# A decoder block whose MLP is computed with seven-product block products: the forms of h2 and z made in the order of the products that read them, the casts of summed weights held back, and the buffers dealt out anew

## The chip, the cores and the metric

The kernel runs on one core of one Trainium2 chip. The metric is the device time of one execution in microseconds (us). Three runs of the kernel before gave 702.37, 704.03 and 705.65 us; their median is 704.03 us. The profile shown here belongs to one further execution, which took 705.45 us by itself.

## The reference, cut to what matters

The input is x with 512 tokens of width 1024, in float32. The first half of the block is a gated merge of differential attention and causal pooling; the change does not touch it. What matters is the end of the layer:

```
x  = x + merged @ w_out                  # 512x1024 @ 1024x1024
h2 = rmsnorm(x, norm_mlp_g)
z  = square(relu(h2 @ w_up))             # 512x1024 @ 1024x4096
x  = x + z @ w_down                      # 512x4096 @ 4096x1024
out = rmsnorm(x, final_norm_g)
```

## The kernel before, in words

**Precision.** Every matrix product is made of three matmuls in the rounded format float32r: each operand is parted into a high part (a cast, made by ScalarE) and a low part (the operand minus its high part, made by VectorE), and hi*hi, hi*lo and lo*hi are added up in PSUM.

**Seven products instead of eight.** The width 4096 of the MLP is taken in four quarters q. For each, `up(q)` multiplies h2 (512 x 1024) by a 1024 x 1024 block of w_up, and `down(q)` multiplies z (512 x 1024) by a 1024 x 1024 block of w_down. Both use a block scheme with seven products of 2x2 blocks in place of eight (Strassen's, in the form with fewer additions). So each operand appears in seven **forms**: for h2 and z these are A11, A12, A22, S1, S2, S3, S4 (S1 to S4 are sums and differences of blocks), for the weights b11, b21, b22 (blocks as they lie in memory) and t1, t2, t3, t4 (sums). The order in which TensorE runs the seven is written out by hand in `up` (lines 702 to 731) and `down` (lines 766 to 778): A11 (m1), then A12 (m2) and S1 (m5) in one order or the other, S2 (m6), S3 (m7), A22 (m4), S4 (m3). Several of them add onto the same two PSUM banks `ma`, with a copy of the banks taken between (`keep`, line 687, on ScalarE in `up`; `to_x1`, line 756, on VectorE in `down`). One product in `up` is 48 matmuls of 256 columns (lines 672, 673, 676), one in `down` is 24 of 512 columns (lines 744 to 746).

**The forms of h2.** Line 580 on: for each of the four token tiles t, w_out's last product is added to x1 (line 560), the row's norm is worked out, h2 is written (line 587), transposed by TensorE (line 593), and its forms are made. Tiles 0 and 1 give A11 and A12; tiles 2 and 3 give, each, A22, S1, S2, S3 and S4 in one go (lines 602 to 611): raw form (`hx`) by ScalarE or VectorE, then `split` (lines 566 and 567) into the high and the low part in `gf`.

**The forms of z.** In `up`, the results of the products are combined into R[0] to R[4] (lines 691 to 730), and `zsplit` (lines 699 and 700) parts each form into `zfh` and `zfl`, two buffers of 28 KB per partition that hold all seven forms. They lie where `hx` and `hbuf` (h2 and its gain) lay before.

**The weights.** `weights` (line 617) is a generator; each product takes its next pair of tiles from it. Raw blocks come by DMA on SyncE's queue into the tiles `wr` (two) and `wal` (two); the sums are built in `wga` (two) and `wal` by VectorE once (line 642) and after that by DMAs that add onto a tile (line 629, issued by GpSimd). `parts` casts a pair to `wh` (ScalarE, line 113) and subtracts for `wl` (VectorE, line 114). `wh` and `wl` have four buffers each, which is two products' worth: a cast for product n has to wait until product n-2 has read its half. For t1, t2 and t4 the same tile `wga` is cast, added to, and cast again.

**Order of the work.** A scheduler places all instructions in each engine's queue at build time, by readiness in a simulated timeline and otherwise by the order of the program; on the chip every engine runs its own queue in that fixed order. `after(a, b)` adds an edge that only places a behind b in that timeline; it is no wait on the chip.

The gain of the last norm is loaded and scaled in `gain` (lines 528 and 529), into the slot that the forms S1 and S2 of h2 leave (line 796).

Of the kernel before, what the change touches and what calls it, by code (L numbers as in the profile page):

```python
# [11 lines left out]
F32 = mybir.dt.float32  # L12
F32R = mybir.dt.float32r
# [39 lines left out]
def block_kernel(ctx, tc, xT, x_tok, gains, pos, consts, w_in, w_v, w_pool, w_out, w_up, w_dn, out):  # L53
# [37 lines left out]
    def f(ap):  # L91
        return ap.bitcast(F32)
# [19 lines left out]
    def split_w(raw, hi, lo, sl=slice(0, 1024), eng=None):  # L112
        ins = A.copy(out=hi[:, sl], in_=raw[:, sl])  # L113
        (eng or G).tensor_tensor(out=lo[:, sl], in0=raw[:, sl], in1=f(hi)[:, sl], op=ALU.subtract)  # L114
        return ins
# [393 lines left out]
    A11, A12, A22, S1, S2, S3, S4 = range(7)  # L509

    x1 = big.tile([P, NT, D], F32, tag="s0", name="x1")
    hbuf = bk.tile([P, 7, 4, HS], F32, tag="zfl", name="hbuf", bufs=1)
    hflat = hbuf.rearrange("p a b c -> p (a b c)")
    h2 = hflat[:, 0 : NT * D].rearrange("p (t d) -> p t d", t=NT)
    hx = bk.tile([P, 7, 4, HS], F32, tag="zfh", name="hx", bufs=1)
    gfs = [big.tile([P, 2, 2, 4, HS], F32R, tag=f"s{i}", name=f"gf{i}") for i in (1, 4, 3)]
    gf7 = bk.tile([P, 1, 2, 4, HS], F32R, name="gf7")
    gf = {}
# [8 lines left out]
    def gain(g, i):  # L527
        nc.sync.dma_start(out=g, in_=gains[i])
        A.mul(out=g, in_=g, mul=-0.5)
        return g  # L530

    def square(t, n, junk):

        A.activation(out=junk, in_=x1[:, t, n * 512 : n * 512 + 512], func=AF.Square, accum_out=st[:, t, n : n + 1])
# [23 lines left out]
    def x1_add(t, n, a_):  # L558
        xs = x1[:, t, n * 512 : n * 512 + 512]
        V.tensor_tensor(out=xs, in0=a_, in1=xs, op=ALU.add)  # L560
        square(t, n, h2[:, t, :512])

    def split(form, sl, src):

        hi, lo = gf[form]
        A.copy(out=hi[:, :, sl], in_=src)  # L566
        V.tensor_tensor(out=lo[:, :, sl], in0=src, in1=f(hi)[:, :, sl], op=ALU.subtract)
# [9 lines left out]
    for t in range(NT):  # L577
        x1_add(t, 0, po[t])
        row_early(t, 0)
    g2b = gain(hflat[:, NT * D : NT * D + D], 0)  # L580
    ws = [get_w(w_out[1, kk], f"o1_{kk}", V if kk % 2 else None) for kk in range(4)]
    for t in range(NT):
        a_ = acc(f"po1_{t}")
        for k in range(NK):
            mm_rows(a_, t, k, ws[k // 2], k == 0, k == NK - 1)
        x1_add(t, 1, a_)
        V.scalar_tensor_tensor(out=h2[:, t], in0=x1[:, t, :], scalar=row_scale(t, 1), in1=g2b, op0=ALU.mult, op1=ALU.mult)
        pv = []
        for b in range(2):
            pt = acc(f"h2T{t}_{b}")  # L590
            for j in range(4):
                k = 4 * b + j
                T.transpose(out=pt[:, j * P : j * P + P], in_=h2[:, t, k * P : k * P + P], identity=ident)
            pv.append(pt.rearrange("p (j q) -> p j q", q=P))
        sl = slice((t % 2) * P, (t % 2) * P + P)
        raw = [hx[:, i, :, sl] for i in range(7)]
        if t < 2:
            for form in (A11, A12):
                A.copy(out=raw[form], in_=pv[form])
                split(form, sl, pv[form])  # L600
        else:
            A.copy(out=raw[A22], in_=pv[1])  # L602
            V.tensor_tensor(out=raw[S1], in0=raw[A22], in1=pv[0], op=ALU.subtract)
            split(S1, sl, raw[S1])
            V.scalar_tensor_tensor(out=raw[S2], in0=raw[S1], scalar=-1.0, in1=raw[A11], op0=ALU.mult, op1=ALU.subtract)
            split(S2, sl, raw[S2])
            V.tensor_tensor(out=raw[S3], in0=raw[A11], in1=pv[0], op=ALU.subtract)  # L607
            split(S3, sl, raw[S3])
            split(A22, sl, raw[A22])
            V.scalar_tensor_tensor(out=raw[S4], in0=raw[S2], scalar=-1.0, in1=raw[A12], op0=ALU.mult, op1=ALU.subtract)  # L610
            split(S4, sl, raw[S4])


    zfh = bk.tile([P, 7, 4, HS], F32R, tag="zfh", name="zfh", bufs=1)
    zfl = bk.tile([P, 7, 4, HS], F32R, tag="zfl", name="zfl", bufs=1)

    def weights(src, q, nm, swap=False):

        def raw(b, tag="wr", pool=wp):
            tiles = [pool.tile([P, 1024], F32, tag=tag, name=f"{tag}_{nm}{b}_{q}_{c}", bufs=2) for c in range(2)]  # L620
            if b is not None:
                for c in range(2):
                    nc.sync.dma_start(out=tiles[c], in_=src[q, b, c])
            return tiles

        def plus(tiles, b):

            for c in range(2):
                G.dma_start(out=tiles[c], in_=src[q, b, c], accum_op=ALU.add)

        def parts(rs, b):
            out_ = []
            for c in range(2):
                hi = wp.tile([P, 1024], F32R, tag="wh", name=f"wh_{nm}{b}_{q}_{c}", bufs=4)
                lo = wp.tile([P, 1024], F32R, tag="wl", name=f"wl_{nm}{b}_{q}_{c}", bufs=4)
                split_w(rs[c], hi, lo, eng=V)
                out_.append((hi, lo))
            return out_

        r11, al, ga = raw(0), raw(1, "wal", bk), raw(None, "wga", bk)  # L640
        for c in range(2):
            V.tensor_tensor(out=ga[c], in0=r11[c], in1=al[c], op=ALU.add)
        yield parts(r11, "b11")
        if swap:
            yield parts(raw(2), "b21")
        plus(al, 3)
        w = parts(ga, "t1")
        plus(ga, 3)
        yield w
        if not swap:  # L650
            yield parts(raw(2), "b21")
        w = parts(ga, "t2")
        plus(ga, 2)
        yield w
        yield parts(al, "t3")
        yield parts(ga, "t4")
        yield parts(raw(3), "b22")

    def up(q):

        W = weights(w_up, q, "u", q == 0)

        def product(form, name, onto=None):
            w, pa = next(W), onto or [acc(f"u{name}{q}_{i}") for i in range(2)]
            rh, rl = gf[form]
            for i in range(2):
                hi, lo = w[i]
                for p in range(2):
                    a_ = pa[i][:, p * HS : p * HS + HS]
                    for k in range(4):  # L670
                        c = slice((p * 4 + k) * P, (p * 4 + k) * P + P)
                        T.matmul(a_, lhsT=hi[:, c], rhs=rh[:, k, :], start=p + k == 0 and onto is None, stop=False, skip_group_check=True)  # L672
                        T.matmul(a_, lhsT=hi[:, c], rhs=rl[:, k, :], start=False, stop=False, skip_group_check=True)  # L673
                    for k in range(4):
                        c = slice((p * 4 + k) * P, (p * 4 + k) * P + P)
                        T.matmul(a_, lhsT=lo[:, c], rhs=rh[:, k, :], start=False, stop=k == 3, skip_group_check=True)  # L676
            return pa
# [18 lines left out]
                A.activation(out=r_, in_=r_, func=AF.Square)  # L696

        def zsplit(form, r):
            A.copy(out=zfh[:, form], in_=r)  # L699
            V.tensor_tensor(out=zfl[:, form], in0=r, in1=f(zfh)[:, form], op=ALU.subtract)  # L700

        ma = product(A11, "m1")
        keep(ma, R[0])
# [12 lines left out]
        z_of(R[1], -1.0)  # L716
        product(A22, "m4", onto=ma)
        z_of(R[3], 1.0, ma)
        V.tensor_tensor(out=R[4], in0=R[0], in1=R[3], op=ALU.subtract)
        V.tensor_tensor(out=R[3], in0=R[1], in1=R[3], op=ALU.subtract)  # L720
        zsplit(S1, R[3])
        V.scalar_tensor_tensor(out=R[0], in0=R[3], scalar=-1.0, in1=R[0], op0=ALU.mult, op1=ALU.subtract)
        product(S4, "m3", onto=mc)
        join(mc, R[2])
        z_of(R[2], -1.0)
        zsplit(A12, R[2])
        zsplit(S2, R[0])
        zsplit(S3, R[4])
        zsplit(A22, R[1])
        V.scalar_tensor_tensor(out=R[2], in0=R[0], scalar=-1.0, in1=R[2], op0=ALU.mult, op1=ALU.subtract)  # L730
        zsplit(S4, R[2])

    def down(q):
        W = weights(w_dn, q, "d")

        def product(form, name, onto=None):

            w, pa = next(W), onto or [acc(f"d{name}{q}_{a}") for a in range(2)]
            for a in range(2):
                for p in range(4):  # L740
                    hi, lo = w[p // 2]
                    sl, tsl = slice((p % 2) * 512, (p % 2) * 512 + 512), slice(a * P, a * P + P)
                    zh, zl = zfh[:, form, p, tsl], zfl[:, form, p, tsl]
                    T.matmul(pa[a], lhsT=zh, rhs=hi[:, sl], start=p == 0 and onto is None, stop=False, skip_group_check=True)  # L744
                    T.matmul(pa[a], lhsT=zl, rhs=hi[:, sl], start=False, stop=False, skip_group_check=True)  # L745
                    T.matmul(pa[a], lhsT=zh, rhs=lo[:, sl], start=False, stop=p == 3, skip_group_check=True)  # L746
            return pa
# [102 lines left out]
```

## Time and profile before

| | |
|---|---|
| three runs | 702.37, 704.03, 705.65 us (median 704.03) |
| the profiled execution | 705.45 us, span from first to last instruction 703.6 us |
| TensorE matmul (PE) busy | 672.5 us, 96% of the span |
| weight loads of TensorE (PEld) | 581.1 us, 83% |
| VectorE (DVE) | 531.8 us, 76% |
| ScalarE (ACT) | 455.3 us, 65% |
| GpSimd (POOL) | 174.5 us, 25% |
| mean granted TensorE clock | 0.989 |
| first matmul of the MLP (line 672) | 357.35 us after the start of the span |
| last matmul | 695.49 us |

PE, DVE, ACT and POOL are the engines; SP is the queue that issues plain DMAs. A row of the timeline has start, duration, engine, line, operation, tiles written and read, shape and count; in square brackets stands how long the engine had been idle and who released it. The end of a matmul in the records is modelled and lies beyond the start of the next one, so the pace of TensorE is read from the distance of two starts, not from the durations.

### The profile page before, as it was taken

To read this page: it belongs to the slowest core of one execution; us is meant where nothing else is said; L and a number is where in the kernel's file an instruction comes from. 1 tells how busy PE (TensorE), PEld (TensorE's weight loads), DVE (VectorE), ACT (ScalarE), POOL (GpSimd) and SP (SyncE) were. 2 spreads that over 40 slices of the span, in tenths; PEclk is the share of its full clock that TensorE was granted. 3 is DMA by queue.
4 is the path that set the end of the run, shared out by engine and by line. 5 is a ranking of instruction groups with operands and counts; after the bars stand their busy time and mean duration, and the time that the engine had idled before them with its cause. 6 is when DMAs were issued, how large, how long until landed. Compare 5 with 4: busy or idle time off the path is not lost.

```text
span 703.6 us, 10026 instructions
## 1 busy us (share of the span) xinstructions
PE 672.5 (96%) x3674; PEld 581.1 (83%) x3674; DVE 531.8 (76%) x852; ACT 455.3 (65%) x735; POOL 174.5 (25%) x167
## 2 busy tenths in 40 slices
PE   9999999999999999999996999999999999999995
PEld 7788788888888887777886987899779987898874
DVE  6953977779798866946588698768966699746995
ACT  7554488986976789565375674368634784366754
POOL 6101634174336434521200010101101010110100
PEclk9999999999999999999998999999999999999998
DMA  8434464335626265254546385786759586595733
GB/s 276 156 117 119 124 146 128 91 88 130 160 71 142 91 143 119 61 216 150 120 128 113 127 195 157 198 221 154 170 156 250 143 206 179 142 231 162 188 88 119
DMA packets 31296, 105.14 MB, mean 149 GB/s; under 512 B 3728, under 2 KB 4368, under 8 KB 31248
## 3 DMA queue, kind: packets, MB, share of 16 engines
q0 software_dynamic: 9792, 35.66, 28.3%
q1 hardware_dynamic: 21456, 68.85, 28.0%
q8 instruction: 29, 0.48, 0.3%
q14 instruction: 19, 0.16, 0.1%
HBM read 102.40 MB, written 2.10 MB: 149 GB/s over the span
## 4 chain that ended last, share of the span: by engine, by line
PE 60%; DVE 15%; DMA 9%; ACT 7%; issue 6%; POOL 2%; SPq 0%; DVEq 0%; ACTq 0%; POOLq 0%
PE um L672 6%; PE um L673 6%; PE um L676 5%; PE dm L745 5%; PE dm L746 4%; PE dm L744 4%; DMA wga_dNone<-w_dn 4%; DVE p L381 2%; PE q L132 2%; PE po L554 2%; PE k L133 2%; PE k L132 2%; PE q L133 2%; PE q L136 2%; PE k L136 2%
## 5 line engine op out<-in xcount | busy, mean ns | idle before, releaser
L672 PE MATMUL um<-gf,wh_ut 128*128 128x256 f32 x256 | 66.4, 291 | 8.0 <-ACT gf L566 6.2
L673 PE MATMUL um<-gf,wh_ut 128*128 128x256 f32 x256 | 66.2, 290 | 0.0
L672 PEld LDWEIGHTS um<-gf,wh_ut 128*128 128x128 f32 x256 | 50.7, 199 | 8.6 <-ACT gf L566 6.6
L745 PE MATMUL dm<-wh_dt,zfl 128*128 128x512 f32 x128 | 50.3, 393 | 3.2 <-DVE zfl L700 3.2
L744 PE MATMUL dm<-wh_dt,zfh 128*128 128x512 f32 x128 | 49.5, 392 | 3.7 <-DVE x L756 3.7
L673 PEld LDWEIGHTS um<-gf,wh_ut 128*128 128x128 f32 x256 | 50.8, 198 | 0.0
L113 ACT CAST wh_ub<-wr_u 128x1024 fp32r<-128x1024 f32 x24 | 25.2, 1054 | 38.1 <-PE dm L745 15.4
L746 PE MATMUL dm<-wl_dt,zfh 128*128 128x512 f32 x128 | 49.2, 390 | 0.0
L672 PE MATMUL um<-gf,wh_ub 128*128 128x256 f32 x192 | 48.1, 283 | 1.1 <-DVE hx L607 1.1
L673 PE MATMUL um<-gf,wh_ub 128*128 128x256 f32 x192 | 48.1, 283 | 0.0
L376 ACT ACTIVATE p<-p,st 128x128 f32<-128x128 f32 (+3 forms) x64 | 35.8, 560 | 17.6 <-DVE st L372 17.1
L113 ACT CAST wh_dt<-wga_dNone 128x1024 fp32r<-128x1024 f32 x24 | 25.3, 1053 | 30.1 <-PE dm L745 14.9
L114 DVE TENSOR_TENSOR wl_ub<-wr_u,wh_ub 128x1024 fp32r<-128x1024 f32 x24 | 29.0, 1223 | 19.7 <-ACT wh_ub L113 19.7
L676 PE MATMUL um<-gf,wl_ut 128*128 128x256 f32 x256 | 42.6, 290 | 0.0
L114 DVE TENSOR_TENSOR wl_ut<-wga_uNone,wh_ut 128x1024 fp32r<-128x1024 f32 x24 | 29.2, 1222 | 17.1 <-ACT wh_ut L113 17.1
L756 DVE TENSOR_TENSOR x<-x,dm 128x512 f32<-128x512 f32 x56 | 37.3, 681 | 6.3 <-PE dm L746 6.3
L113 ACT CAST wh_ut<-wga_uNone 128x1024 fp32r<-128x1024 f32 x24 | 25.1, 1048 | 24.4 <-DMA wga_uNone<-w_up 14.4
L672 PEld LDWEIGHTS um<-gf,wh_ub 128*128 128x128 f32 x192 | 36.8, 192 | 1.4 <-ACT hx L602 1.2
L700 DVE TENSOR_TENSOR zfl<-rawz,zfh 128x1024 fp32r<-128x1024 f32 x28 | 34.1, 1220 | 4.2 <-ACT zfh L699 4.1
L673 PEld LDWEIGHTS um<-gf,wh_ub 128*128 128x128 f32 x192 | 36.8, 192 | 0.2
L676 PEld LDWEIGHTS um<-gf,wl_ut 128*128 128x128 f32 x256 | 36.9, 200 | 0.0
L744 PE MATMUL dm<-wh_db,zfh 128*128 128x512 f32 x96 | 36.8, 390 | 0.0
(279 smaller groups left out, 2114.6 us busy)
## 6 DMA issues: line engine op xcount, KB each, us to landing
wr_u<-w_up SPq DMA_DIRECT2D x24, 512.0 KB, 5.3
wr_d<-w_dn SPq DMA_DIRECT2D x24, 512.0 KB, 3.8
wga_uNone<-w_up POOLq DMA_DIRECT2D x16, 512.0 KB, 6.0
wga_dNone<-w_dn POOLq DMA_DIRECT2D x16, 512.0 KB, 6.0
wr_q<-w_in SPq DMA_DIRECT2D x8, 512.0 KB, 3.2
wr_k<-w_in SPq DMA_DIRECT2D x8, 512.0 KB, 3.3
wr_ga<-w_in SPq DMA_DIRECT2D x8, 512.0 KB, 3.2
wr_gp<-w_in SPq DMA_DIRECT2D x8, 512.0 KB, 3.3
```

What stands on the lines that cost most here:

```text
L113: ins = A.copy(out=hi[:, sl], in_=raw[:, sl])
L114: (eng or G).tensor_tensor(out=lo[:, sl], in0=raw[:, sl], in1=f(hi)[:, sl], op=ALU.subtract)
L132: T.matmul(acc, lhsT=hi[:, c], rhs=rh[:, k, :], start=k == 0, stop=False)
L376: A.activation(out=pr[:, c, :N], in_=pr[:, c, :N], func=AF.Exp, scale=-1.0, bias=st[:, c : c + 1], accum_out=st[:, 2 + c : 3 + c])
L672: T.matmul(a_, lhsT=hi[:, c], rhs=rh[:, k, :], start=p + k == 0 and onto is None, stop=False, skip_group_check=True)
L673: T.matmul(a_, lhsT=hi[:, c], rhs=rl[:, k, :], start=False, stop=False, skip_group_check=True)
L676: T.matmul(a_, lhsT=lo[:, c], rhs=rh[:, k, :], start=False, stop=k == 3, skip_group_check=True)
L700: V.tensor_tensor(out=zfl[:, form], in0=r, in1=f(zfh)[:, form], op=ALU.subtract)
L744: T.matmul(pa[a], lhsT=zh, rhs=hi[:, sl], start=p == 0 and onto is None, stop=False, skip_group_check=True)
L745: T.matmul(pa[a], lhsT=zl, rhs=hi[:, sl], start=False, stop=False, skip_group_check=True)
L746: T.matmul(pa[a], lhsT=zh, rhs=lo[:, sl], start=False, stop=p == 3, skip_group_check=True)
L756: V.tensor_tensor(out=xs, in0=xs, in1=pa[a], op=(ALU.add, ALU.subtract)[n])
```

## The change

It does five things.

1. `hx` and h2 become five tiles of one tag `zf` (8 KB each); h2 holds two token tiles at a time, and the gain g2b lies in a free half of the fourth. In the loop over t, tiles 2 and 3 make only A22 (raw), S1 with its split, and S3 (raw). A new function `form_h2` makes the splits of S2, S3 and A22, and the raw form and split of S4 and S2, right ahead of the product that reads the form, in `up(0)` alone.
2. `zfh` and `zfl` are gone. `zsplit` takes a tile from the same ring `zf` of five for each form, and works in two halves of 512 columns.
3. In `up`, the form S1 of z is made first, in halves, straight into R[4]; S3 (R[0]-R[3]), which stood ahead of it, is made after S2.
4. Every third pair of weight parts lies in two further tiles (`whb`, `wlb`), so that parts for three products exist at once.
5. The casts of t2, t3 and t4 get an edge behind the first matmul of the latest product that has begun in the program (`hold`).

```
+    def zf(name, dt=F32R):
+        return bk.tile([P, 2, 4, HS], dt, tag="zf", name=name, bufs=5)
+
+    hxs = [zf(f"hx{i}", F32) for i in range(4)]
+    h2 = zf("h2", F32).rearrange("p a b c -> p a (b c)")
+    hx = {form: hxs[i // 2][:, i % 2] for i, form in enumerate((A11, A12, A22, S1, S2, S4, S3))}
...
             V.tensor_tensor(out=raw[S1], in0=raw[A22], in1=pv[0], op=ALU.subtract)
             split(S1, sl, raw[S1])
-            V.scalar_tensor_tensor(out=raw[S2], in0=raw[S1], scalar=-1.0, in1=raw[A11], op0=ALU.mult, op1=ALU.subtract)
-            split(S2, sl, raw[S2])
             V.tensor_tensor(out=raw[S3], in0=raw[A11], in1=pv[0], op=ALU.subtract)
-            split(S3, sl, raw[S3])
-            split(A22, sl, raw[A22])
-            V.scalar_tensor_tensor(out=raw[S4], in0=raw[S2], scalar=-1.0, in1=raw[A12], op0=ALU.mult, op1=ALU.subtract)
-            split(S4, sl, raw[S4])
+
+    def form_h2(form):
+
+        for t in range(2):
+            sl = slice(t * P, t * P + P)
+            raw = {i: hx[i][:, :, sl] for i in hx}
+            if form == S2:
+                V.scalar_tensor_tensor(out=raw[S2], in0=raw[S1], scalar=-1.0, in1=raw[A11], op0=ALU.mult, op1=ALU.subtract)
+            if form == S4:
+                V.scalar_tensor_tensor(out=raw[S4], in0=raw[S2], scalar=-1.0, in1=raw[A12], op0=ALU.mult, op1=ALU.subtract)
+            if form in (S2, S3, A22, S4):
+                split(form, sl, raw[form])
...
-        def parts(rs, b):
+        def parts(rs, b, hold=None):
+
+            third = nparts[0] % 3 == 2
+            nparts[0] += 1
...
+                cast = split_w(rs[c], hi, lo, eng=V)
+                if hold:
+                    after(cast, hold)
...
-        w = parts(ga, "t2")
+        w = parts(ga, "t2", first[-1])
         plus(ga, 2)
         yield w
-        yield parts(al, "t3")
-        yield parts(ga, "t4")
+        yield parts(al, "t3", first[-1])
+        yield parts(ga, "t4", first[-1])
...
         def zsplit(form, r):
-            A.copy(out=zfh[:, form], in_=r)
-            V.tensor_tensor(out=zfl[:, form], in0=r, in1=f(zfh)[:, form], op=ALU.subtract)
+            z = zform[form] = zf(f"z{form}_{q}")
+            for i, r_ in enumerate(halves(r)):
+                hi, lo = (z[:, j, 2 * i : 2 * i + 2, :] for j in range(2))
+                A.copy(out=hi, in_=r_)
+                V.tensor_tensor(out=lo, in0=r_, in1=f(hi), op=ALU.subtract)
...
-        V.tensor_tensor(out=R[4], in0=R[0], in1=R[3], op=ALU.subtract)
-        V.tensor_tensor(out=R[3], in0=R[1], in1=R[3], op=ALU.subtract)
-        zsplit(S1, R[3])
-        V.scalar_tensor_tensor(out=R[0], in0=R[3], scalar=-1.0, in1=R[0], op0=ALU.mult, op1=ALU.subtract)
+        for a_, b_, c_ in zip(halves(R[4]), halves(R[1]), halves(R[3])):
+            V.tensor_tensor(out=a_, in0=b_, in1=c_, op=ALU.subtract)
+        zsplit(S1, R[4])
         product(S4, "m3", onto=mc)
         join(mc, R[2])
         z_of(R[2], -1.0)
         zsplit(A12, R[2])
-        zsplit(S2, R[0])
-        zsplit(S3, R[4])
+        V.scalar_tensor_tensor(out=R[4], in0=R[4], scalar=-1.0, in1=R[0], op0=ALU.mult, op1=ALU.subtract)
+        zsplit(S2, R[4])
+        V.tensor_tensor(out=R[0], in0=R[0], in1=R[3], op=ALU.subtract)
+        zsplit(S3, R[0])
         zsplit(A22, R[1])
```

## The prediction on record

> **What bounds the kernel now.** I read the page first, then the waits of TensorE, then its timeline at those places, then the queues of ScalarE and VectorE around them.
>
> ```profile
> span 703.6 us, 10026 instructions
> PEclk9999999999999999999998999999999999999998
> ```
>
> ```profile
> PE um L672 <- ACT gf L566: 6.2, 2, 3.9
> PE dm L744 <- DVE x L756: 3.7, 4, 1.1
> PE dm L745 <- DVE zfl L700: 3.2, 4, 0.8
> PE um L672 <- ACT rawz L687: 1.7, 1, 1.7
> PE um L672 <- DVE hx L607: 1.1, 1, 1.1
> ```
>
> The second line is the granted clock in tenths over 40 slices of the span; it drops in one slice behind the middle, and in the last, where TensorE has ended. The waits (total us, times, longest) hold all that TensorE loses in the MLP: five causes, and everything the diff touches is among their releasers. How much each costs is seen from starts:
>
> ```profile
> 357.35 0.28 PE L672 MATMUL um<-gf,wh_ub 128*128 128x256 f32 x1
> 367.51 0.36 PE L676 MATMUL um<-gf,wl_ub 128*128 128x256 f32 x1
> 368.94 0.36 PE L672 MATMUL um<-gf,wh_ub 128*128 128x256 f32 x1 [1.07 <-DVE hx L607]
> 371.41 0.64 PE L676 MATMUL um<-gf,wl_ub 128*128 128x256 f32 x4
> 374.34 0.50 PE L672 MATMUL um<-gf,wh_ut 128*128 128x256 f32 x2 [2.29 <-ACT gf L566]
> 378.77 0.80 PE L672 MATMUL um<-gf,wh_ut 128*128 128x256 f32 x2 [3.93 <-ACT gf L566]
> 415.64 0.62 PE L744 MATMUL dm<-wh_db,zfh 128*128 128x512 f32 x2
> 417.10 0.50 PE L745 MATMUL dm<-wh_dt,zfl 128*128 128x512 f32 x1 [0.84 <-DVE zfl L700]
> 432.19 0.39 PE L745 MATMUL dm<-wh_dt,zfl 128*128 128x512 f32 x1
> 432.42 0.39 PE L746 MATMUL dm<-wl_dt,zfh 128*128 128x512 f32 x1
> 433.77 0.47 PE L744 MATMUL dm<-wh_dt,zfh 128*128 128x512 f32 x1 [0.96 <-DVE x L756]
> 639.97 0.28 PE L673 MATMUL um<-gf,wh_ut 128*128 128x256 f32 x1
> 640.09 0.64 PE L676 MATMUL um<-gf,wl_ut 128*128 128x256 f32 x4
> 642.47 0.39 PE L672 MATMUL um<-gf,wh_ut 128*128 128x256 f32 x1 [1.75 <-ACT rawz L687]
> 695.49 0.39 PE L746 MATMUL dm<-wl_db,zfh 128*128 128x512 f32 x1
> ```
>
> A matmul of 256 columns starts every 0.12 us (639.97 to 640.09), one of 512 every 0.23 us (432.19 to 432.42; 0.227 over a run of them). So the MLP's pure work is 28 products x 48 x 0.12 = 161.3 us in the four `up` and 28 x 24 x 0.227 = 152.5 us in the four `down`, together 313.8 us. It ran from 357.35 to 695.72 us, 338.4 us. Of the rest, 16 transposes of h2, put at the same 0.12 us each, are 1.9 us. About 22.7 us are lost. TensorE is the bound, and nothing that leaves it these 313.8 us can win more than that.
>
> The loss in five parts, as distance of two starts less one pace:
> - Head, first gap: 368.94 - 367.51 - 0.12 = 1.31 us.
> - Head, second gap: the last of the four matmuls at 371.41 starts at 371.77; until 378.77 only two more start: 7.00 - 3 x 0.12 = 6.64 us.
> - From A11 to S1 in `down`: 417.10 - 415.87 - 0.23 = 1.00, which is 0.16 more than the idle time in the row. Four such waits: 3.2 + 4 x 0.16 = 3.8 us.
> - From S2 to S3 in `down`: 433.77 - 432.42 - 0.23 = 1.12, again 0.16 more. Four: 3.7 + 0.6 = 4.3 us.
> - In the last `up`: 642.47 - 640.45 - 0.12 = 1.90 us.
>
> Two of the gaps cost clock as well (columns: stretch, its length, then busy us and instructions of PE, PEld, DVE, ACT, POOL, then granted clock, DMA share, GB/s):
>
> ```profile
> 371.90:378.70 6.80, 0.65 (x4) 0.30 (x2) 6.80 (x10) 5.19 (x9) 0.86 (x1) 0.89 0.54 96
> 378.70:384.10 5.40, 5.33 (x25) 5.33 (x26) 3.19 (x6) 2.54 (x6) 0.86 (x1) 0.51 0.85 152
> 642.40:647.00 4.60, 4.53 (x25) 4.53 (x26) 3.65 (x4) 3.24 (x6) 0.10 (x1) 0.63 0.29 98
> 415.00:435.00 20.00, 18.20 (x80) 14.37 (x78) 19.51 (x21) 9.78 (x10) 1.73 (x2) 1.00 0.74 189
> ```
>
> After the head's gap the clock is 0.51 and 25 matmuls take 5.4 us in place of 25 x 0.12 = 3.0: 2.4 us. After 642.4 a mean of 0.63 over 4.6 us means 3.4 us at half rate, so 1.7 us. Sum: head 1.3 + 6.6 + 2.4 = 10.3; inside `down` 3.8 + 4.3 = 8.1; the last `up` 1.9 + 1.7 = 3.6. Together 22.0, which fits the 22.7.
>
> **The change part by part.** Why the gaps are there:
>
> ```profile
> 365.25 2.35 DVE L114 TENSOR_TENSOR wl_ut<-wga_uNone,wh_ut 128x1024 fp32r<-128x1024 f32 x2
> 369.92 0.68 DVE L603 TENSOR_TENSOR hx<-hx,h2T 128x512 f32<-128x512 f32 x1
> 372.20 1.04 ACT L113 CAST wh_ut<-wga_uNone 128x1024 fp32r<-128x1024 f32 x1 [2.13 <-DMA wga_uNone<-w_up]
> 376.12 1.04 ACT L113 CAST wh_ut<-wga_uNone 128x1024 fp32r<-128x1024 f32 x1 [1.31 <-DMA wga_uNone<-w_up]
> 430.72 1.05 ACT L113 CAST wh_dt<-wga_dNone 128x1024 fp32r<-128x1024 f32 x1 [2.44 <-DMA wga_dNone<-w_dn]
> 431.80 1.23 DVE L114 TENSOR_TENSOR wl_dt<-wga_dNone,wh_dt 128x1024 fp32r<-128x1024 f32 x1 [0.40 <-ACT wh_dt L113]
> 432.94 1.28 DVE L756 TENSOR_TENSOR x<-x,dm 128x512 f32<-128x512 f32 x2
> 408.96 1.22 DVE L719 TENSOR_TENSOR rawz<-rawz 128x1024 f32<-128x1024 f32 x1
> 410.69 1.22 DVE L720 TENSOR_TENSOR rawz<-rawz 128x1024 f32<-128x1024 f32 x1
> 415.83 1.22 DVE L700 TENSOR_TENSOR zfl<-rawz,zfh 128x1024 fp32r<-128x1024 f32 x1
> 640.89 1.06 ACT L529 ACTIVATE gfb<-gfb 128x1024 f32<-128x1024 f32 x1 [2.44 <-DMA gfb<-gains]
> ```
>
> *Held casts, head.* S1 of the fourth token tile exists raw at 369.92 + 0.68 = 370.6. ScalarE could cast it at once, but stands 2.13 us and again 1.31 us on two casts of t2 whose DMA has not landed; the form's casts lie behind them. With the edge, t2's casts come behind S1's first matmul. Cast and subtraction (0.6 and 0.7 us, a little over half of the rows of 1024 columns) then end at about 372, as A12's matmuls run out at 371.9. The second gap goes but for some tenths, and the half rate with it: 6.6 + 2.4 us. What is late next is t2 itself: cast 1.04 and 1.23 of subtraction per half. Its first half landed at 372.2, so is ready by 374.5; the second landed at 376.1, ready at 378.4. S2 would start at 371.9 + 5.8 = 377.7 and needs the second half at 380.5. It fits by 2 us.
>
> *Later splits.* S2's two raw forms and two splits on VectorE, 4 x 0.68, now stand between S1's first matmul and S2 (5.8 us, in which t2 takes 2 x 1.2 more): 5.1 us, covered with 0.7 us to spare, and by 2.9 us more for t2's second half. S3, A22 and S4 each need 1.4 to 2.7 us in 5.8. Cost 0; without cover TensorE stands for whatever is over 5.8 us.
>
> *First gap of the head.* It ends with line 607 of tile 2, which frees a PSUM bank; the order of VectorE had put 2.35 us of t1's subtraction (365.25) before it. t1 is the third pair, gets the new tiles, and need not wait until A11 is read. So its cast and subtraction move ahead, and 1.3 us go. Bounds: 0 to 1.3 of gain; and those 2.35 us must go somewhere among the norm's rows before 357, where they can delay h2 by up to one subtraction, 1.2 us. I take the whole gain and 0.5 of cost.
>
> *S2 to S3 in `down`.* VectorE stands behind t4's subtraction (431.80), this behind its cast, this 2.44 us behind the DMA; `to_x1`, which frees the bank, begins at 432.94. With the edge, t4's cast is placed behind S3's first matmul, and so behind `to_x1`. Four times gone: 4.3 us. Queued behind a late cast are then its own subtraction and A22, one product (24 x 0.227 = 5.4 us) later; two casts and two subtractions in series need 1.05 + 2 x 1.23 = 3.5 us. Covered.
>
> *A11 to S1 in `down`.* VectorE made S3's difference (408.96) before S1's (410.69), and S1's low part at 415.83. Now S1's is first, by halves: 1.22 us less ahead, the first half need not wait for the second square, and the third tile pair moves t1's subtractions of `down` one product forward. TensorE needs it at 415.9, it came at 417.05. 1.2 us are enough; all four gaps go, 3.8 us.
>
> *Halves.* Two ops of 512 columns take 1.28 us on VectorE (432.94) against 1.22 for one of 1024: 0.06 x 8 = 0.5 us per quarter. ScalarE is busy under half of 415 to 435. Hidden; without cover 2 us in all.
>
> *The ring of five.* z's A22 and S4 wait for A11 and S1 of `down` to be read; they are used four to five products later, over 20 us. h2's two halves: tile 2 waits for tile 0's transposes, a product earlier. Cost 0. Raw DMAs on SyncE's queue and the adding DMAs on GpSimd's are as many as before, some up to a product earlier.
>
> *The gain gfb.* Untouched, so I leave its 3.6 us in: a scale that waits 2.44 us for its DMA stands ahead of `keep` on ScalarE.
>
> Sum: -10.3 - 8.1 + 0.5 = -17.9 us. On the profiled execution 705.45 - 17.9 = 687.5; that execution lies 1.4 above the median, so **686.0 us** against 704.0.
>
> **The rivals.**
> - *The gain's stall goes as well.* Between S2 and S3 ScalarE now has t4's and b22's casts ready, so the scale may be placed behind the first `keep`. For: the row at 640.89 is a matter of place alone. Against: nothing orders it. 686.0 - 3.6 = 682.4. Chance 0.18.
> - *The head is only half mended.* VectorE is busy 6.80 of 6.80 us there, so S1 or S2 may still come 3 us late. Then the gap is 3.0 and the half rate of 2.4 us stays: 686.0 + 5.4 = 691.4. For the clock: 642.47 shows that a gap of 1.9 us is followed by half rate. Chance 0.12. The Trainium skill, TensorE: Matmul & The Clock Gate, section on why this matters, allows gaps up to about 3 us without a drop. By that rule such a rest would cost its 3.0 us alone, 689.0; the trace disagrees, with 3.4 us at half rate behind 1.9 us.
> - *VectorE is the bound where `up` meets `down`.* It is busy 19.51 of 20 us in 415 to 435, and the halves add to it. If S1 comes as late as now and the 0.5 us per quarter show, 3.8 + 2.0 come back: 691.8. Against: the reordering takes 1.22 us from ahead of S1, the halves put 0.2 there. Chance 0.07. The Trainium skill, Perfetto Trace Analysis, section on optimizing Scalar/DVE operations, says to group operations where the engine is saturated and to break them up where it only causes bubbles; VectorE is here both.
> - *The edge does little.* It orders a simulated timeline; if DMAs land there as early as before relative to the products, the casts stay in front of the same instructions. Then only the 3.8 us go: 700.2, no change. Against: the edge hangs on the product, not on the DMA. Chance 0.06.
> - *Slower: raw casts block `keep`.* With three pairs of tiles, casts of b21 and b22 are no longer held back by TensorE's reading, but stand in ScalarE's queue as soon as the simulated DMA lands. Where the real one is over 2.3 us late (half a product, 2.9, less the copy, 0.6), `keep` is late and TensorE stops, as at 640.89, for 3.6 us. Twice in each of four `up`: 686.0 + 8 x 3.6 = 714.8; it turns slower than before from six such stops on. For: the row of the gain. Against: raw blocks are asked for a product earlier. Chance 0.07.
>
> **How the numbers follow.** The forecast has 0.50. About 0.5%, 3.5 us, is what a measurement can tell from no change. Faster: 0.50 + 0.18 + 0.12 + 0.07 = 0.87; same 0.06; slower 0.07. The range takes in the first four cases, 682.4 to 691.8. Below, it gets the scatter of the runs shown (1.7 us) and the 0.5 that I charged: 680. Above, 1.7 of scatter, 0.7 more for t1 and 1.3 for the first gap: 696.
>
> **What would show it.** Right: no wait of line 672 on the casts of h2's forms over 1 us, clock 1.00 from 357 to 640; no waits on z's low part or on `to_x1` in `down`; the first matmul of `up` to the last of `down` in about 320 us (338.4 - 10.3 - 8.1); the stop behind the gain still there. Wrong: ScalarE idle on a DMA with a copy or a split behind it in the queue; new rows of TensorE waiting on `wh` or `wl`; the norm's rows before 357 later by more than 1 us.

## The result, and the profile after

The changed kernel took 711.53 us (median of four runs, 709.98 to 712.71) against 703.90 us (702.37 to 705.65) for the kernel before on the same chip: a ratio of 1.0106, 95% interval 1.0073 to 1.0139. It is about 7.6 us slower, where 18 us of gain were forecast. Its profiled execution took 710.68 us with a span of 708.7 us. The profile of the kernel before comes from an execution of 705.45 us, above its median, so the two profiles differ by 5.2 us and not by 7.6. Lines of the changed kernel are numbered anew: matmuls of `up` 692, 694, 697, of `down` 770, 772, 773; `keep` 708, `z_of` 716 and 717, the two halves of `zsplit` 723 and 724, `to_x1` 783, `split` 569 and 570.

The page of the changed kernel, span and granted clock:

```profile
span 708.7 us, 10061 instructions
PEclk9999999999999999999999999999999999999988
```

Its waits of TensorE in the MLP (total us, times, longest):

```profile
PE dm L770 <- DVE st L542: 4.8, 1, 4.8
PE um L692 <- ACT rawz L708: 3.7, 3, 2.2
PE dm L770 <- DVE x L783: 2.9, 1, 2.9
PE um L694 <- DVE gf L570: 2.6, 1, 2.6
PE dm L772 <- DVE z L724: 1.3, 1, 1.3
PE um L697 <- DVE wl_ut L114: 0.9, 1, 0.9
PE um L692 <- ACT gf L569: 0.8, 1, 0.8
PE dm L773 <- DVE wl_dt L114: 0.4, 1, 0.4
```

The eight regular waits in `down` (four on z's low part, four on `to_x1`) are gone from this list, and so is the stop behind the gain. In their place stand single stops, fewer and longer. The rows at which TensorE resumes, and the stretches behind three of them (columns of the second fence as in the prediction):

```profile
371.38 0.50 PE L692 MATMUL um<-gf,wh_ut 128*128 128x256 f32 x2 [0.77 <-ACT gf L569]
374.51 0.58 PE L694 MATMUL um<-gf,wh_ut 128*128 128x256 f32 x1 [2.62 <-DVE gf L570]
508.76 0.50 PE L770 MATMUL dm<-wh_dt,z 128*128 128x512 f32 x1 [2.90 <-DVE x L783]
554.07 0.38 PE L692 MATMUL um<-gf,wh_ut 128*128 128x256 f32 x1 [2.18 <-ACT rawz L708]
663.24 0.50 PE L772 MATMUL dm<-wh_db,z 128*128 128x512 f32 x1 [1.31 <-DVE z L724]
679.75 0.76 PE L770 MATMUL dm<-wh_dt,z 128*128 128x512 f32 x1 [4.79 <-DVE st L542]
```

```profile
374.20:377.70 3.50, 3.19 (x15) 3.19 (x16) 3.50 (x6) 3.47 (x8) 0.01 (x1) 0.51 0.00 0
555.10:558.60 3.50, 3.50 (x19) 3.50 (x18) 2.38 (x4) 2.17 (x3) 0.00 (x0) 0.51 0.79 267
679.50:685.00 5.50, 5.25 (x13) 4.18 (x14) 4.42 (x10) 4.10 (x6) 0.00 (x0) 0.51 0.00 0
```

Each stop again costs some 0.16 us more than the idle time in its row. The head: 0.93 + 2.78, and half of 3.2 us at half rate, 1.6: 5.3 us, where there had been 10.3. In `down`: 3.06 + 1.47 + 0.56 + 4.95, and half of 5.25 us, 2.6: 12.6 us, where there had been 8.1. In `up`: `keep` 3.7 + 3 x 0.16, the low part of t1 0.9 + 0.16, and half of 3.5 us, 1.75: 7.0 us, where there had been 3.6. That is 2.9 us more than before, and the measured stretch from the first matmul (357.22) to the last (698.36) agrees: 341.1 us against 338.1. The other 2.2 us of the span come behind the last matmul (10.3 us against 8.1), because the last two products now end together and three `to_x1` fall due at once:

```profile
697.42 2.05 DVE L783 TENSOR_TENSOR x<-x,dm 128x512 f32<-128x512 f32 x3 [2.36 <-PE dm L773]
```

So the stops that were aimed at did go. The question is who made the new ones. ScalarE's queue at the start of the last `down`, then VectorE's:

```profile
652.60 0.63 ACT L716 ACTIVATE rawz<-rawz 128x512 f32<-128x512 f32 x1
659.14 1.05 ACT L113 CAST wh_db<-wr_d 128x1024 fp32r<-128x1024 f32 x1 [5.90 <-DMA wr_d<-w_dn]
660.09 0.63 ACT L717 ACTIVATE rawz<-rawz 128x512 f32<-128x512 f32 x1
660.75 0.62 ACT L723 CAST z<-rawz 128x512 fp32r<-128x512 f32 x1
```

```profile
660.22 1.23 DVE L114 TENSOR_TENSOR wl_db<-wr_d,wh_db 128x1024 fp32r<-128x1024 f32 x1 [4.72 <-ACT wh_db L113]
...
677.19 1.22 DVE L114 TENSOR_TENSOR wl_dt<-wal_d,wh_dt 128x1024 fp32r<-128x1024 f32 x1
678.33 1.27 DVE L783 TENSOR_TENSOR x<-x,dm 128x512 f32<-128x512 f32 x2
```

A raw cast (b21, whose tile is `wr_d`) stands between the relu (line 716) and the square (line 717) of one half of z and waits 5.90 us for its block. Everything behind it in ScalarE's queue waits too: z's square, z's casts. VectorE waits 4.72 us for the same cast and then has no pause until `to_x1` at 678.33, which TensorE had wanted at 674.8. (The row at which TensorE resumes names line 542, a small instruction of the last norm right behind `to_x1` in VectorE's queue; the second of the two `to_x1` ends at 679.60, and TensorE starts 0.15 us later.) The stop that ended at 508.76 has the same history: a raw cast waited 2.91 us until 488.24, VectorE 2.14 us for it, and VectorE had no pause from there to the `to_x1` that was late. In the kernel before the same casts stand behind z's work and wait for nothing:

```profile
658.39 1.99 ACT L699 CAST zfh<-rawz 128x1024 fp32r<-128x1024 f32 x2
660.28 1.99 ACT L113 CAST wh_db<-wr_d 128x1024 fp32r<-128x1024 f32 x2
```

ScalarE's waits for these blocks, in the list of the kernel before (there is no such row for `wh_db`) and then in that of the changed one:

```profile
ACT wh_ub L113 <- DMA wr_u<-w_up: 13.1, 4, 4.3
```

```profile
ACT wh_ub L113 <- DMA wr_u<-w_up: 38.7, 10, 9.8
ACT wh_db L113 <- DMA wr_d<-w_dn: 18.7, 10, 5.9
```

### The profile page after: what moved, and what is told of

Its sections match the earlier page's. It is cut to its first block, busy times and chain, and to the rows that moved or that the text cites. A ratio compares the mean times of both kernels' runs of the same rounds, so it can differ in the third digit from the quotient of the medians.

```text
span 708.7 us, 10061 instructions
## 1 busy us (share of the span) xinstructions
PE 674.0 (95%) x3674; PEld 582.9 (82%) x3674; DVE 530.4 (75%) x884; ACT 455.9 (64%) x763; POOL 174.3 (25%) x167
## 4 chain that ended last, share of the span: by engine, by line
PE 52%; DVE 20%; DMA 10%; ACT 8%; issue 7%; POOL 2%; SPq 0%; DVEq 0%; ACTq 0%; POOLq 0%
PE dm L770 5%; PE dm L772 5%; PE dm L773 4%; PE um L694 4%; PE um L697 4%; PE um L692 4%; DMA wr_u<-w_up 4%; DMA wga_uNone<-w_up 2%; DMA wr_d<-w_dn 2%; DVE p L381 2%; PE q L132 2%; PE k L133 2%; PE k L132 2%; PE q L133 2%; PE q L136 2%
## 5 line engine op out<-in xcount | busy, mean ns | idle before, releaser
L770 PE MATMUL dm<-wh_dt,z 128*128 128x512 f32 x128 | 50.9, 399 | 7.7 <-DVE st L542 4.8
L113 ACT CAST wh_ub<-wr_u 128x1024 fp32r<-128x1024 f32 x24 | 25.1, 1053 | 49.5 <-DMA wr_u<-w_up 38.7
L773 PE MATMUL dm<-wl_dt,z 128*128 128x512 f32 x128 | 50.5, 397 | 0.4 <-DVE wl_dt L114 0.4
L772 PE MATMUL dm<-wh_dt,z 128*128 128x512 f32 x128 | 50.8, 397 | 0.0
L113 ACT CAST wh_db<-wr_d 128x1024 fp32r<-128x1024 f32 x24 | 25.1, 1050 | 29.7 <-DMA wr_d<-w_dn 18.7
L772 PE MATMUL dm<-wh_db,z 128*128 128x512 f32 x96 | 37.5, 391 | 1.3 <-DVE z L724 1.3
L770 PE MATMUL dm<-wh_db,z 128*128 128x512 f32 x96 | 37.4, 391 | 0.0
```

What stands on the lines that cost most here:

```text
L770: m = T.matmul(pa[a], lhsT=zh, rhs=hi[:, sl], start=p == 0 and onto is None, stop=False, skip_group_check=True)
```

## The experiments

Theory A: with the third pair of tiles, TensorE's reading no longer holds back the raw casts; they stand early in ScalarE's queue, wait there for late blocks, and hold up whatever lies behind. Theory B: VectorE is full where `up` meets `down`, so that work moved there comes back as a late `to_x1`. The times (medians in us, ratio to the kernel before in the same series):

| | time | ratio, 95% interval |
|---|---|---|
| e1, two pairs | 698.60 | 0.9924 (0.9905 to 0.9943) |
| e2, all casts held | 713.06 | 1.0136 (1.0090 to 1.0183) |
| e3, none held | 721.73 | 1.0271 (1.0235 to 1.0306) |
| e4, before with t2, t3, t4 held | 696.75 | 0.9901 (0.9880 to 0.9921) |
| e5, e4 with S1 first | 695.62 | 0.9909 (0.9895 to 0.9924) |
| e6, e5 with t3 on GpSimd | 706.05 | 1.0063 (1.0047 to 1.0080) |
| e7, e1 with t3 on GpSimd | 713.37 | 1.0153 (1.0111 to 1.0194) |
| e8, e2 with t3 on GpSimd | 720.22 | 1.0266 (1.0233 to 1.0300) |
| e9, e1 relieved | 696.59 | 0.9913 (0.9885 to 0.9940) |
| e10, e2 relieved | 699.33 | 0.9953 (0.9933 to 0.9972) |
| e11, raw blocks there | 695.59 | 0.9898 (0.9871 to 0.9925) |
| e12, changed kernel relieved | 707.62 | 1.0057 (1.0033 to 1.0082) |

**e1: the third pair alone undone.**

```diff
-            third = nparts[0] % 3 == 2
+            third = False
```

> The changed kernel with the third pair of weight tiles taken out: all parts lie in the four wh and four wl tiles again; ring of five, order of the forms and held casts stay. Theory A (the third pair lets casts of raw blocks stand early in ScalarE's queue, where they wait for DMAs that land late, and the work behind them is late): the casts wait again for TensorE's reading, ScalarE's waits on raw DMAs fall from 57 us (38.7 + 18.7) to some 15 to 25, the three long stops inside down and the late copies in up go; 684 to 694 us. Theory B (VectorE is overloaded where up meets down, by z in halves and the new order): nothing of that depends on the third pair; 706 to 713 us.

698.6 us. The third pair costs about 13 us, and without it the rest of the change is a gain. It stays above the range of theory A: in `down` TensorE still waits for `to_x1`, and there VectorE has no free moment in 27 us:

```profile
PE dm L770 <- DVE x L783: 4.4, 3, 1.5
```

```profile
405.00:432.00 27.00, 25.52 (x122) 21.18 (x121) 27.00 (x36) 18.07 (x26) 3.45 (x4) 1.00 0.80 191
```

**e2: every cast gets the edge, the third pair stays.**

```diff
         def parts(rs, b, hold=None):
+            hold = hold or (first[-1] if first else None)
```

> The changed kernel with the third pair kept, but every cast of weights, raw blocks and t1 too, has the edge behind the first matmul of the latest product. Theory A: it is the place of the raw casts in the queue that costs, not the tiles, so 684 to 696 us, about as without the third pair. Theory B: 706 to 713 us. If it is slow and the version without the third pair is fast, the tiles themselves (which pair waits for which product) are to blame.

713.1 us: theory A as I had stated it failed here. The stops behind raw casts went, but four others of 3.45, 3.65, 4.13 and 5.58 us came, one in each `down`, all from S2 to S3, at a late `to_x1`. (For three of them the profile names a raw cast, which ended at about the same time; in all four TensorE starts 0.14 us after the end of a `to_x1`.) ScalarE still waited 27.9 + 7.4 us for raw blocks, where it had been 38.7 + 18.7. That the tiles themselves are to blame, as the expectation has it for this outcome, is ruled out by e10 and e11 below, which keep the tiles and are faster than the kernel before.

**e3: no edge at all, third pair kept.**

```diff
-                if hold:
+                if False:
                     after(cast, hold)
```

> The changed kernel with the edges of t2, t3 and t4 taken out, everything else kept. Theory A: casts of sums join the raw casts in standing early before late DMAs; 711 us or more, up to 722. Theory B: about as now, 707 to 715 us. A rival, that the edges themselves do the damage: below 705 us.

721.7 us: the edges are worth 1.6%, about 11 us, to the changed kernel. Without them `keep` is late by up to 7.2 us:

```profile
PE um L692 <- ACT rawz L708: 14.7, 3, 7.2
```

**e4: the kernel before with nothing but the edges.**

```diff
...
-        w = parts(ga, "t2")
+        w = parts(ga, "t2", first[-1])
...
-        yield parts(al, "t3")
-        yield parts(ga, "t4")
+        yield parts(al, "t3", first[-1])
+        yield parts(ga, "t4", first[-1])
```

> The kernel before with the edges on the casts of t2, t3 and t4 alone. Theory A, and the prediction's reading of the stops before: the wait of S3 in down on to_x1 (3.7 us in four) goes, and in the head the casts of h2's forms no longer stand behind t2's, which is worth some 3 to 6 us; the stop behind the gain (3.6 us) and the wait on z's low part (3.2) stay; 693 to 699 us. If the edges do the damage: 704 us or more.

696.75 us, as expected. The edge alone takes three of the four waits on `to_x1`, and z's waits stay:

```profile
PE dm L753 <- DVE zfl L706: 3.3, 4, 0.8
...
PE dm L751 <- DVE x L764: 0.8, 1, 0.8
```

All that e1 has beside the edges (form order of h2, ring, z's order, halves) brings no gain that shows: its ratio is 0.9924, that of the edges alone 0.9901.

**e5: e4 with S1 of z made ahead of S3, in whole operations.**

```diff
-        V.tensor_tensor(out=R[4], in0=R[0], in1=R[3], op=ALU.subtract)
-        V.tensor_tensor(out=R[3], in0=R[1], in1=R[3], op=ALU.subtract)
-        zsplit(S1, R[3])
+        V.tensor_tensor(out=R[4], in0=R[1], in1=R[3], op=ALU.subtract)
+        zsplit(S1, R[4])
+        V.tensor_tensor(out=R[3], in0=R[0], in1=R[3], op=ALU.subtract)
...
-        zsplit(S3, R[4])
+        zsplit(S3, R[3])
```

> The kernel before with the held casts of t2, t3 and t4 (696.75 us in its own run) and, beside that, S1's difference of z made ahead of S3's, nothing else (no halves, no third pair). Theory A (VectorE has room, only the place of an instruction in the queues decides): the four waits of 0.9 to 1.0 us from A11 to S1 go, 692.5 to 693.5. Theory B (VectorE is full from the end of `up` to the fourth product of `down`, so what is moved ahead comes back behind): the four waits go, but `to_x1` gets later at S2 to S3 by about as much, 695.5 to 697.

695.6 us, and no measurable step from e4. The waits on `zfl` are gone and `to_x1` is late instead:

```profile
PE dm L751 <- DVE x L764: 2.2, 5, 0.5
PE dm L751 <- DVE st L539: 0.4, 1, 0.4
```

The idle time on `zfl`, 3.3 us, went, and that on `to_x1` grew from 0.8 to 2.6 us; VectorE is busy 29.29 of the 30 us from 400 to 430. That fits theory B: most of the wait was moved, not removed.

**e6, e7, e8: t3's subtractions of `down` on GpSimd**, in e5, e1 and e2.

```diff
-                cast = split_w(rs[c], hi, lo, eng=V)
+                cast = split_w(rs[c], hi, lo, eng=G if nm + b == "dt3" else V)
```

> As the run before, with the two subtractions of t3 in each `down` on GpSimd in place of VectorE (2 x 1.14 us less on VectorE, 2 x about 2.5 us on GpSimd, which is idle there). Theory B: neither the waits from A11 to S1 nor those from S2 to S3 are there, 692 to 693.5, faster than the run before by 2 to 4 us. Theory A: no change against the run before; if GpSimd's subtractions come late, waits on t3's low part appear and it is slower.

> The changed kernel with two pairs (698.6 us in its own run) and t3's subtractions of `down` on GpSimd. Theory B: its stops from S2 to S3 (3 x 1.64 and 1.16, 6.1 us) go, about 692.5. Theory A: they stay, 698 to 699.

> The changed kernel with the third pair and all casts held (713.1 us in its own run) and t3's subtractions of `down` on GpSimd. Theory B: its stops from S2 to S3 (3.45, 3.65, 4.13, 5.58: 16.8 us) come from a full VectorE, so they shrink by at least 2.3 us each, to 704 or less, and by all if the queue catches up, 696. Theory A (ScalarE's waits on late transfers hold the queue): they stay, 711 to 714.

All three got slower, by 1.3 to 2.3%, which neither theory had expected (theory A allowed for it only with waits on t3's low part, and there are none). In e6, GpSimd's rows and then VectorE's:

```profile
420.45 2.40 POOL L114 TENSOR_TENSOR wl_dt<-wal_d,wh_dt 128x1024 fp32r<-128x1024 f32 x1 [11.22 <-ACT wh_dt L113]
...
423.42 2.77 POOL L114 TENSOR_TENSOR wl_dt<-wal_d,wh_dt 128x1024 fp32r<-128x1024 f32 x1
```

```profile
418.87 1.22 DVE L114 TENSOR_TENSOR wl_dt<-wga_dNone,wh_dt 128x1024 fp32r<-128x1024 f32 x1
...
420.60 3.34 DVE L114 TENSOR_TENSOR wl_dt<-wga_dNone,wh_dt 128x1024 fp32r<-128x1024 f32 x1
423.86 0.67 DVE L764 TENSOR_TENSOR x<-x,dm 128x512 f32<-128x512 f32 x1
424.46 2.82 DVE L706 TENSOR_TENSOR zfl<-rawz,zfh 128x1024 fp32r<-128x1024 f32 x1
```

The same subtraction on VectorE takes 1.22 us alone and 3.34 us beside GpSimd's: it ends about 1.1 us after GpSimd's has ended. `to_x1`, whose second operand lies in PSUM, ran beside GpSimd's second one in its usual 0.67 us. So VectorE was freed of 2 x 1.14 us and lost 2.1 + 1.6 us: 1.4 us more load in each `down`, and the waits on `to_x1` grew from 2.6 us in all to 8.2, with half rates behind them (mean granted clock 0.988 against 0.995):

```profile
PE dm L751 <- DVE x L764: 8.2, 4, 2.6
```

The Trainium skill, SBUF — State Buffer, section on the two separate sides, says this: a VectorE operation with two inputs in SBUF and a GpSimd operation that reads SBUF exclude each other for the whole instruction. The rows agree. In e8 the waits from S2 to S3 grew as well, from 16.2 us of idle time in e2 to 23.0. e7 became slower in another way: the stops from S2 to S3 went in three `down` of four, as theory B said, but TensorE now stopped for a half of t4:

```profile
PE dm L770 <- ACT wh_dt L113: 9.3, 3, 4.2
```

GpSimd also issues the DMAs that add onto t4's tile, and they stand in its queue behind its own subtractions. In the first `down` of e7 the two subtractions took 8.12 us, and the last of these DMAs was issued at 430.86 us; in e1 it was issued at 425.35. So the move to GpSimd had two costs, and the three runs by themselves neither show nor refute theory B.

**e9, e10, e12: VectorE relieved without loading another engine**, in e1, e2 and the changed kernel.

```diff
-                cast = split_w(rs[c], hi, lo, eng=V)
+                if nm + b == "dt3":
+                    cast, lo = A.copy(out=hi, in_=rs[c]), hi
+                else:
+                    cast = split_w(rs[c], hi, lo, eng=V)
```

The relieved kernels leave out the low parts of t3 in `down`, so they serve for the time alone.

> The changed kernel with two pairs (698.6 us in its own run), and t3's low parts in `down` not computed (its products take the high part in their place): VectorE has two subtractions of 1.14 us less in each `down` and no other engine has more. Theory B (VectorE is full up to S3 of `down`): the stops from S2 to S3 (1.64 three times, 1.16) go, 692 to 693.5. Theory A (VectorE has room): no change, 698 to 699.

> The changed kernel with the third pair and all casts held (713.1 us), with the same relief of VectorE. Theory B: its stops of 3.45, 3.65, 4.13 and 5.58 us shrink by 2.3 us each or more, 704 or less. If they stay (711 to 714), something other than VectorE's load holds `to_x1` there: the order of the queues alone.

> The changed kernel with the relief of VectorE alone (t3's low parts in `down` not computed). Theory A: `keep` and z's casts are still late behind the raw casts; only what VectorE has to catch up gets shorter, 704 to 709. Theory B: the loss goes, 698 or less.

e10 fell by 1.8%, about 13 us, to 699.3: its four stops shrank by 1.8 to 2.3 us each. What had held e2 was VectorE, and theory B holds there (t3's tiles also come free one subtraction earlier, which no run parts from the relief). e12 fell by 0.5% only, 3 to 4 us, to 707.6, in the range that theory A gave: the changed kernel is not held by VectorE's load in the first place. e9 did neither: 2 us lower by the median, 0.1% by the ratio. Its stops from S2 to S3 went, but a product later VectorE waited 3.39 us for the cast of a half of t4, whose sum was late by itself, and `to_x1` lay behind it. ScalarE's row there:

```profile
433.35 1.05 ACT L113 CAST wh_dt<-wga_dNone 128x1024 fp32r<-128x1024 f32 x1 [5.56 <-DMA wga_dNone<-w_dn]
```

**e11: the raw casts take a block that has long been there.**

```diff
+        def there(b):
+            tiles = raw(b)
+            return tiles if nm == "u" and q == 0 else [f(gf[A11][1]).rearrange("p b c -> p (b c)")] * 2
...
-            yield parts(raw(2), "b21")
+            yield parts(there(2), "b21")
...
-        yield parts(raw(3), "b22")
+        yield parts(there(3), "b22")
```

This kernel multiplies by another block in place of b21 and b22, so it too serves for the time alone.

> The changed kernel, whose casts of b21 and b22 (except b21 and b22 of the first `up`) take another block that has long been in memory, so that they wait for no transfer; the transfers themselves run as before. Theory A (raw casts that stand in ScalarE's queue waiting for late transfers hold `keep` and z's casts, and with these VectorE): the stops behind them go, 690 to 698. Theory B (VectorE is full whatever ScalarE does): the third pair still costs, 705 to 712.

695.6 us, 2.1% or about 15 us below the changed kernel, with the same third pair and the same places: the raw cast still stands between z's squares and z's casts, now without a wait. All that TensorE still waits for in the MLP:

```profile
PE um L696 <- ACT rawz L712: 3.1, 3, 1.5
PE um L698 <- DVE gf L570: 2.6, 1, 2.6
PE um L696 <- ACT gf L569: 0.7, 1, 0.7
```

No row of `down` is left; the stops at `keep` stay, 3.1 us against 3.7. The last `down` in e11, then in the changed kernel:

```profile
645.00:681.00 36.00, 36.00 (x169) 30.19 (x169) 33.69 (x53) 22.25 (x39) 1.73 (x2) 1.00 0.35 77
```

```profile
645.00:681.00 36.00, 29.45 (x150) 24.45 (x150) 30.15 (x43) 21.58 (x34) 4.31 (x5) 0.96 0.58 133
```

VectorE is busier in e11 (33.69 us against 30.15) and TensorE never stops. So it is the waiting that cost the time in `down`. One reserve: with no reader of their own the raw tiles come free sooner in e11, so the transfers themselves run earlier too.

## Why the prediction was wrong

The forecast of 686.0 us gave a sum of -17.9; the result lies on the other side, by the mechanism of the rival that was given 0.07. By its steps:

- **"The ring of five ... Cost 0. Raw DMAs ... are as many as before, some up to a product earlier."** This is the step that failed, with the third pair costed only as a gain. I looked at what the pair allows (casts a product earlier) and not at what had kept the casts in order: in the kernel before, the casts of raw blocks waited mostly until TensorE had read the tile that they write (15.4 + 9.4 + 11.9 + 2.5 = 39.2 us), and 13.1 us for transfers. In the changed kernel they waited 5.7 + 5.1 + 10.6 + 0.3 = 21.7 us for TensorE and 38.7 + 18.7 = 57.4 us for transfers. From the first `down` on the raw blocks were asked for earlier too, by 3 to 15 us on the clock, but not everywhere by as much as the casts. In the last `down`, where TensorE itself was 4.1 us ahead of the kernel before, the second block of b21 was asked for at 649.66 us, right after VectorE had made the low part that freed its tile, and in the kernel before at 652.84. Its cast was next in ScalarE's queue at 653.24, and in the kernel before it ran at about 661.2. The block landed at about 659.1. Longer transfers are not the cause by themselves: the median from issue to landing rose from 3.8 to 6.5 us for the raw blocks of w_down and fell from 5.3 to 4.4 for those of w_up, and e11 has 6.8 and 4.6 without the loss. Why the scheduler placed the casts so early is not shown, as its simulated timeline is not on record.

That the pair is the loss is shown by e1 (-13 us without the pair) and e11 (-15 us with the pair and no wait).
- **The rival "raw casts block `keep`".** Its cause was right, its place was not. It had eight stops of 3.6 us at `keep`; there were three, of 3.7 us in all, and these are not shown to come from raw casts. In e11, where ScalarE waits only 3.0 us in all for raw blocks, 3.1 us of them stay (e1, without the third pair, has 0.7), and ahead of the longest, which ended at 554.07, ScalarE had fallen behind at a cast of t2:

```profile
539.32 1.05 ACT L113 CAST wh_ut<-wga_uNone 128x1024 fp32r<-128x1024 f32 x1 [7.44 <-DMA wga_uNone<-w_up]
```

The dearer stops came by a way that I had not drawn: raw cast, z's squares and casts behind it, VectorE idle and then behindhand, `to_x1` late. Its "against", raw blocks asked for a product earlier, held in part only.
- **Held casts.** Right in kind: e3 and e4 give the edge 11 and 7 us. It is the part of the change that pays.
- **Head.** Forecast: all 10.3 us go. 5.3 stayed. It is the rival "only half mended", whose rest was 5.4: VectorE was full there, and S2's raw forms, a `join` and a part of z stood ahead of S1's last split. In e1, which has the later splits and no third pair, the head's waits are no shorter than in e4, which has the edge alone (rows below); so the later splits brought nothing that shows.

```profile
PE um L694 <- DVE gf L570: 2.5, 2, 1.4
PE um L692 <- DVE hx L608: 1.8, 1, 1.8
...
PE um L692 <- ACT gf L569: 0.9, 1, 0.9
```

```profile
PE um L679 <- DVE gf L567: 2.6, 1, 2.6
PE um L677 <- ACT gf L566: 1.2, 1, 1.2
```

- **A11 to S1.** The four waits went, as said. But e5 shows that in a kernel without the third pair this is worth nothing measurable: VectorE is nearly full there, and most of the wait comes back at S2 to S3. It is what the rival with VectorE as the bound said, in another place.
- **S2 to S3.** The regular waits went, also as said; in two of the four `down` larger ones took their place.
- **The gain.** I left its 3.6 us in; it went, as the rival with 0.18 had it. ScalarE now reaches the scale after the transfer has landed.

Not settled: why e2's VectorE falls further behind than e1's with the same work. The relief shows that it is VectorE, not which of its moved instructions. In e2 VectorE also paused in `down` for b21's cast (1.11 us until 410.69, 2.32 us until 663.44) and is busy 25.89 us in the 27 us from 405 to 432, so a part of theory A may be left in it.

## What to carry to other kernels

A shortage of buffers also keeps queues in order: before adding buffers, ask which instruction it was that could not stand early, what it will wait for once it can, and what lies behind it on its engine. Where an engine is full over a stretch, moving its work within the stretch moves the wait; look for what can leave it, and check in the rows whether the instructions of the two engines slow each other down, and what else stands in the queue of the engine that takes the work. Of a change in several parts, try the cheap one alone: the edges by themselves (e4) gave 696.75 us, faster than both kernels.

## What the runs showed of the hardware

- GpSimd and VectorE stood in each other's way whole instructions at a time, as told under e6: 1.22 us became 3.34 and 2.82 us, and an operation with an operand in PSUM kept its 0.67 us.
- The clock. The stop that ended at 554.07 lasted 2.34 us and half rate followed; the one that ended at 508.76 lasted 3.06 us, and none did:

```profile
508.70:513.00 4.30, 4.24 (x19) 3.51 (x20) 4.30 (x6) 0.00 (x0) 0.00 (x0) 1.00 0.83 243
```

The length of a stop alone doesn't decide. The Trainium skill, TensorE: Matmul & The Clock Gate, section on what is actually happening, speaks of a window of about 3.4 us that runs freely; that would fit both rows, and no run here tested it. The same page of the Trainium skill, section on why this matters, allows stops of up to about 3 us, which the 2.34 us speak against.
